# A feed-forward in written order: operands of a unit as one paced stream, weights that skip steps, low parts one step behind high parts

## The chip, the cores and the metric

The kernel runs on one core of one Trainium2 chip. The metric is the device time of one execution in microseconds. TensorE (PE) multiplies matrices; ScalarE (ACT), VectorE (DVE) and GpSimd (POOL) work on rows; SyncE (SP) issues the transfers (DMA). Each engine takes its instructions in the order in which they stand.

## What is computed

One layer of an encoder for 2048 prompt tokens and 32 sample tokens (2080 in all, 1024 channels): a mixing sub-layer (band attention beside gated linear attention), then a gated feed-forward with a causal convolution. All of the change lies in the feed-forward, which fills roughly the last 44% of the time:

```python
D_MODEL = 1024; D_FF = 2816; CONV_W = 3
...
def conv_ffn(h, conv_state, w_up, w_dw, b_dw, w_down):
    t = h.shape[1]
    u = h @ w_up                                       # (t, 2 * D_FF)
    uu = jnp.concatenate([conv_state.astype(u.dtype), u], axis=1)
    y = b_dw
    for j in range(CONV_W):
        y = y + w_dw[j] * uu[:, j:j + t]
    a, g = jnp.split(y, 2, axis=-1)
    out = (jax.nn.gelu(a, approximate=True) * g) @ w_down
    return out, uu[:, -(CONV_W - 1):]
```

All is float32.

## The kernel before

**Numbers in two parts.** A float32 operand is split into a high part (a copy rounded to a shorter format, made by ACT) and a low part (what is left, made by DVE as operand minus high part). A product is the sum of high·high, high·low and low·high on PE.

**Units and blocks.** The tokens are cut into three pairs of segments of about 348. The feed-forward has twelve *units*: u0, u1, u2 are the up-projection of one pair each, with 22 *blocks* of 128 channels; u3 to u11 are the down-projection, three groups for each pair, with 4 blocks each. A block is a 2×2 product done with seven multiplications (Strassen's scheme in Winograd's form). Its weights are named A11, S2, S1, S3, A12, S4, A22 and its operands (rows of tokens) B11, T2, T1, T3, B21, B22, T4; the S and T are sums of quarters. Each of the seven has four inner tiles of 128 (three in u5, u8 and u11) by three matmuls, so 12 (9) matmuls. The operands are the same for all blocks of a unit, the weights are new for each block.

**Steps.** After each multiplication `block` calls `side()`, a *step*. A step first runs what was put off until now (`run_due`), then makes one half of an operand of the next unit (`hstep`), then one of the coming weights (`next(wq)`), and a second if there is room in the ring of weights; last it drives the final part of an earlier pair (`pend`). The product A22·T4 of a block is written after A11·B11 of the next block.

**Order.** From the third block of u0 on, `in_order[0]` is true, and PE, ACT, DVE, POOL and SP take instructions in the order in which this Python code writes them. `put(n, f)` puts a piece of work off by n + 1 steps. So a high part is written in one step (L1464 for operands, L1540 for weights), and its low part (L1465, L1543) two steps later.

**Operands.** `load_ops` is a generator: it issues loads three halves ahead (L1323, L1440, L1444, L1447) into a few raw tiles `ht`, and each time that it is resumed it makes one high part and puts the low part off. The loads, from `h2T` and its sums `hT` (up) or from `actD` and its sums `aT` (down), wait on SP until a raw tile is free, which is once the low part was made from it. Operands of the next unit were asked for in three pieces:

```python
ahead_ = {14: [0], 17: [1], 21: range(2, 7)} if grp is None else {1: [0], 2: [1], 3: range(2, 7)}
if m in ahead_:
    hq.append(load_ops([(u + 1, OPS[i]) for i in ahead_[m]]))
```

that is B11 in block 14, T2 in block 17 and the other five in the last block (down-projection: blocks 1, 2 and 3).

**Weights.** `weights` loads quarters or stored sums (L1518) into ten raw slots, makes the high part, puts off the low part. In u0 and u3 to u5 the weights are *fresh*: the sums S are made on the chip, three on POOL (L1522) and S4 on DVE, and stored (L1546) for the later pairs.

**Rest.** L1597 is the matmul. L1705, L1713 and L1716 are ACT's copies of the results of A11·B11, S2·T2 (to U2) and S1·T1; L1719 and L1727 are DVE's additions after S3·T3 and S4·B22. L1612 and L1614 are the convolution. L1624 to L1627 (`act_sums`) make the T sums of the activations in every second block, L1647 multiplies by the gate, L1629 and L1648 store them. L1817 and L1821 are the last multiplication and addition of the output of an earlier pair, in u6 and u9.

Of the kernel before, what the change touches and what calls it, by code (L numbers as in the profile page):

```python
# [58 lines left out]
def encoder_step(ctx: ExitStack, tc: tile.TileContext, I, O):  # L59
# [1363 lines left out]
    def put(n, f):  # L1423

        later(n, f) if n and in_order[0] else f()

    def load_ops(todo):

        raws = {}

        def load(i):
            u, x, j, n = todo[i]
            p, g = UNITS[u]
            w = WIDTH[u]
            raws[i] = r = h_tile()
            if g is None and x in HB:
                k, s = HB[x]
                load_h(r, [(y, 4 * k + j + y, 2 * p + s) for y in range(2)], w)
            elif g is None:
                nc.sync.dma_start(r[:, :, :w], dap(hT, ((4 * p + HT[x]) * 512 + 128 * j) * W,  # L1440
                                                   [[W, 128], [128 * W, 2], [1, w]]))
            elif x in HB:
                k, s = HB[x]
                nc.sync.dma_start(r[:, :n, :w], dap(actD, ((p * MF + 8 * g + 2 * j + k) * 256 + s) * SEG,  # L1444
                                                    [[2 * SEG, 128], [512 * SEG, n], [1, w]]))
            else:
                nc.sync.dma_start(r[:, :n, :w], dap(aT, ((4 * p + HT[x]) * 11 + 4 * g + j) * 128 * SEG,  # L1447
                                                    [[SEG, 128], [128 * SEG, n], [1, w]]))

        todo = [(u, x, j, min(2, NK[u] - j)) for u, x in todo for j in (0, 2)]  # L1450
        for i in range(min(3, len(todo))):
            load(i)
        yield
        for i, (u, x, j, n) in enumerate(todo):
            if i + 3 < len(todo):
                load(i + 3)
            at = (7 * u + OPS.index(x)) % len(HP)
            assert HLIVE.setdefault(at, (u, x)) == (u, x)
            hi, lo = HP[at]
            if j:  # L1460
                put(1, lambda at=at, u=u, x=x: HO.update({(u, x): HP[at]}))
            w = WIDTH[u]
            hi, lo, r = hi[:, j:j + n, :w], lo[:, j:j + n, :w], raws.pop(i)[:, :n, :w]
            nc.scalar.activation(hi, r, AF.Copy)  # L1464
            put(1, lambda hi=hi, lo=lo, r=r: nc.vector.tensor_sub(lo, r, f32(hi)))  # L1465
            yield


# [2 lines left out]
    LIVE = {}  # L1471
# [33 lines left out]
    def weights():  # L1505
# [25 lines left out]
        def part(c, x, i):  # L1531
            u, m = cols[c]
            while True:
                place = ring((u, m, x))
                if place:
                    break
                yield
            n = NK[u]
            hi, lo = place
            nc.scalar.activation(hi[:, :n], raw(i, n), AF.Copy)  # L1540

            def low():
                nc.vector.tensor_sub(lo[:, :n], raw(i, n), f32(hi[:, :n]))  # L1543
                WO[u, m, x] = place
                if fresh[c] and x in SUM:
                    nc.sync.dma_start(w_rows(u, m, x), raw(i, n))  # L1546
                if fresh[c] and x == "A12":

                    def total4():
                        total(c, nc.vector, "tensor_sub", i, i, at[c, "S2"])  # L1550
                        at[c, "S4"] = i

                    put(1, total4)
                elif fresh[c] and x == "S2":
                    put(4, lambda: free.append(at.pop((c, "S2"))))
                else:
                    put(3 if fresh[c] and x in SUM else 1, lambda: free.append(i))

            put(1, low)

        fetch()
        for cur in range(len(cols)):
# [79 lines left out]
    def up_g(p, m, x, y, before):  # L1642

        o, c, d = WP[p] - 2, m + MF, int(p == 2)

        def act():
            nc.vector.tensor_mul(y[:, :, :o], y[:, :, :o], YG[:, :, :o])  # L1647
            put(2, lambda: nc.sync.dma_start(actD[p, m, :, :, :o], y[:, :, :o]))  # L1648
            if m % 2:
                made.append((p, m // 2, before, y))  # L1650

        if d:
            put(1, lambda: conv_outputs(x[:, 1], c))
        put(d + 1, lambda: tap(2, YG, x, c, o))
        put(d + 2, lambda: tap(1, YG, x, c, o))
        put(d + 3, lambda: tap(0, YG, x, c, o))
        put(d + 4, act)
# [171 lines left out]

            put(2, store)  # L1830

    pending = []

    def pend():
        while pending and next(pending[0], 1) == 1:
            pending.pop(0)
# [35 lines left out]
    YG = work[:, 8 * W:10 * W].rearrange("p (x w) -> p x w", w=W)  # L1872
    P5, U2 = work[:, 10 * W:11 * W], work[:, 11 * W:12 * W]

    def side():
        run_due()
        step()
        hstep()
        next(wq, None)
        if in_order[0] and len(LIVE) < len(RING) - 1:  # L1880

            next(wq, None)
        pend()
# [3 lines left out]
    for u, (p, grp) in enumerate(UNITS):  # L1887
        for m in range(NM[u]):
            if u == 0 and m >= 2 and ndone[0] == NBLK:
                ndone[0] += 1  # L1890
            if u + 1 < len(UNITS):

                ahead_ = {14: [0], 17: [1], 21: range(2, 7)} if grp is None else {1: [0], 2: [1], 3: range(2, 7)}
                if m in ahead_:
                    hq.append(load_ops([(u + 1, OPS[i]) for i in ahead_[m]]))
            if u == 3 and m == 1:
                nc.sync.dma_start(O["conv"], uc)
            if u == len(UNITS) - 1 and m == 2:
# [96 lines left out]
```

## Time and profile before

| | |
|---|---|
| median of 3 runs | 3315.63 us (3313.65 to 3321.91) |
| the profiled execution | 3320.35 us, its span 3318.4 us |
| PE busy | 3133.5 us, 94% of the span |
| DVE busy | 2269.8 us, 68% |
| ACT busy | 1650.5 us, 50% |
| POOL busy | 586.3 us, 18% |
| granted PE clock over the span | 0.979 |
| feed-forward | about 1850 to 3291 us of the span |

The shares are averages over the whole span; what an engine does in the feed-forward is read from its stretches. "Gap" below is time in which PE runs no matmul. An arrow in a row of waits means "waited for".

### The profile page before, as it was taken

How to read it: one execution, taken by the hardware profiler on the slowest of the kernel's cores; microseconds unless marked ns; L12 is line 12 of the kernel's file. 1: busy time of each engine (PE TensorE's matmuls, PEld its weight loads, DVE VectorE, ACT ScalarE, POOL GpSimd, SP SyncE). 2: the span in 40 equal slices, each digit the busy share in tenths (PEclk: the TensorE clock that was granted, in tenths of full speed). 3: DMA queues.
4: the chain of work that ended last, by engine and by line, in shares of the span. 5: the costliest groups of instructions: out<-in, count | busy, mean ns of one | idle time of the engine just before them, and what ended most of it. 6: DMA issues, size and time to landing. Idle time of an engine off the chain costs nothing. (4 is left out here: it accounts for less than half of the span.)

```text
span 3318.4 us, 57469 instructions
## 1 busy us (share of the span) xinstructions
PE 3133.5 (94%) x19928; PEld 2985.6 (90%) x19928; DVE 2269.8 (68%) x4858; ACT 1650.5 (50%) x3835; POOL 586.3 (18%) x687
## 2 busy tenths in 40 slices
PE   6999999999999999999999799999999999989996
PEld 4889998888999999889988789999999999989996
DVE  6725526674555555654776888987878788887876
ACT  4412224443544555543544645555555556575755
POOL 3102101111111111111444423300000001411011
PEclk9999999999999999999999899999999999999998
DMA  7344434445333333664575686676676666777774
GB/s 216 112 123 135 132 111 119 129 125 138 108 109 108 111 110 106 196 185 150 165 211 159 217 265 221 220 229 192 196 209 206 192 206 212 254 241 241 240 245 150
DMA packets 601365, 580.21 MB, mean 175 GB/s; under 512 B 55761, under 2 KB 529570, under 8 KB 601074
## 3 DMA queue, kind: packets, MB, share of 16 engines
q1 hardware_dynamic: 556386, 528.93, 53.2%
q10 hardware_dynamic: 44432, 47.34, 4.5%
q8 instruction: 157, 2.57, 0.3%
q14 instruction: 134, 1.10, 0.1%
q0 software_dynamic: 256, 0.26, 0.0%
HBM read 388.71 MB, written 187.65 MB: 174 GB/s over the span
## 5 line engine op out<-in xcount | busy, mean ns | idle before, releaser
L1597 PE MATMUL ad<-hA,hB 128*128 128x350 f32 (+2 forms) x1800 | 315.0, 325 | 9.3 <-DVE hB L1543 7.8
L1597 PEld LDWEIGHTS ad<-hA,hB 128*128 128x128 f32 x1800 | 294.6, 190 | 12.1 <-DVE hB L1543 9.2
L78 PE MATMUL pm<-hA,wh 128*128 128x416 f32 x768 | 288.8, 376 | 0.0
L1543 DVE TENSOR_TENSOR hA<-raws,hA 128x512 fp32r<-128x512 f32 (+1 forms) x360 | 270.1, 761 | 4.0 <-PE po L79 2.2
L79 PE MATMUL pm<-hA,wh 128*128 128x416 f32 x768 | 270.0, 352 | 0.0
L80 PE MATMUL pm<-hA,wl 128*128 128x416 f32 x768 | 269.8, 351 | 0.0
L1540 ACT ACTIVATE hA<-raws 128x512 fp32r<-128x512 f32 (+1 forms) x360 | 216.5, 615 | 54.7 <-PE ad L1597 13.8
L1597 PE MATMUL ad<-hA,hA 128*128 128x348 f32 (+2 forms) x1122 | 198.8, 328 | 9.7 <-DVE hA L1543 8.0
L938 POOL TENSOR_SCALAR P<-P,mx 128x640 f32<-128x640 f32 (+5 forms) x136 | 101.3, 745 | 546.5 <-DVE mx L937 260.9
L1597 PEld LDWEIGHTS ad<-hA,hA 128*128 128x128 f32 x1122 | 185.5, 192 | 11.8 <-DVE hA L1543 8.9
L1543 DVE TENSOR_TENSOR hB<-raws,hB 128x512 fp32r<-128x512 f32 (+1 forms) x269 | 196.1, 739 | 0.0
L1522 POOL TENSOR_TENSOR raws<-raws 128x512 f32<-128x512 f32 (+1 forms) x70 | 111.0, 1597 | 467.7 <-DVE hA L1543 347.7
L1597 PE MATMUL g<-hA,hB 128*128 128x348 f32 (+2 forms) x987 | 176.6, 329 | 18.1 <-ACT work L1713 11.0
L1597 PE MATMUL ad<-hA 128*128 128x350 f32 (+2 forms) x1101 | 191.1, 323 | 2.3 <-ACT work L1716 2.1
L1597 PEld LDWEIGHTS g<-hA,hB 128*128 128x128 f32 x987 | 163.5, 193 | 21.6 <-ACT work L1713 13.3
L1597 PEld LDWEIGHTS ad<-hA 128*128 128x128 f32 x1101 | 178.7, 189 | 3.9 <-ACT work L1716 3.6
L1705 ACT COPY g<-ad 128x348 f32<-128x348 f32 (+2 forms) x102 | 44.4, 435 | 276.9 <-PE ad L1597 230.2
L1540 ACT ACTIVATE hB<-raws 128x512 fp32r<-128x512 f32 (+1 forms) x269 | 163.3, 616 | 32.9 <-DVE raws L1522 14.2
L78 PE MATMUL pn<-wh,hA 128*128 128x256 f32 (+1 forms) x624 | 177.8, 285 | 0.0
L79 PE MATMUL pn<-wl,hA 128*128 128x256 f32 (+1 forms) x624 | 176.9, 283 | 0.0
L80 PE MATMUL pn<-wh,hA 128*128 128x256 f32 (+1 forms) x624 | 176.8, 283 | 0.0
L69 ACT ACTIVATE pth<-pp 128x256 fp32r<-128x256 f32 (+1 forms) x288 | 106.1, 373 | 127.0 <-PE pp L1005 115.8
(439 smaller groups left out, 9093.8 us busy)
## 6 DMA issues: line engine op xcount, KB each, us to landing
raws<-in_w_up_dram SPq DMA_DIRECT2D x220, 256.0 KB, 4.6
raws<-sW SPq DMA_DIRECT2D x176, 256.0 KB, 4.3
sW<-raws SPq DMA_DIRECT2D x88, 256.0 KB, 3.4
raws<-in_w_down_dram SPq DMA_DIRECT2D x80, 256.0 KB, 5.2
wr<-in_w_in_dram SPq DMA_DIRECT2D x76, 256.0 KB, 3.4
sgT<-tx ACTq DMA_DIRECT2D x80, 208.0 KB, 2.4
wa<-in_w_ada_dram SPq DMA_DIRECT2D x64, 256.0 KB, 3.0
keys<-ks SPq DMA_DIRECT2D x128, 128.0 KB, 2.9
```

The lines of the kernel that those rows point to most:

```text
L69: i = nc.scalar.activation(hi, src, AF.Copy)
L78: nc.tensor.matmul(out, ah, bh, start=first and i == 0, stop=False)
L79: nc.tensor.matmul(out, ah, bl, start=False, stop=False)
L80: nc.tensor.matmul(out, al, bh, start=False, stop=last and i == n - 1)
L938: nc.gpsimd.tensor_scalar(P[:m, :tot], P[:m, :tot], mx[:m, 6:7], 1.0, op0=OP.mult, op1=OP.mult)
L1522: getattr(eng, op)(raw(out, n), raw(a, n), raw(b, n))
L1540: nc.scalar.activation(hi[:, :n], raw(i, n), AF.Copy)
L1543: nc.vector.tensor_sub(lo[:, :n], raw(i, n), f32(hi[:, :n]))
L1597: nc.tensor.matmul(out[:, :w], l_[:, k], r_[:, k, :w], start=first and k == 0 and i == 0, stop=k == n - 1 and i == 2, skip_group_check=True)
L1705: nc.scalar.copy(g[:, 0, :w], ad[:, 0, :w])
```

## The change

Four things change, all in the order of instructions. `soon(n, f)` puts work off by one step less than `put(n, f)`, and the low parts of operands and weights, the sum S4, the freeing of raw slots and the store of activations now use it. `load_ops` is called once for each unit, for all seven operands, at block 18 of an up-projection and block 1 of a down-projection; it keeps two or three loads ahead, starts three steps after its first loads, makes two halves in three steps, and lets a step pass where the place of an operand is not yet free. `side()` makes no weight in every second step that made a half, if more than four weights are held, and no second weight in a step that made a half.

```diff
+    pending = []
+    made_half = [False]
+
+    def soon(n, f):
+
+        later(n - 1, f) if in_order[0] else f()
+
     def load_ops(todo):
...
         todo = [(u, x, j, min(2, NK[u] - j)) for u, x in todo for j in (0, 2)]
-        for i in range(min(3, len(todo))):
-            load(i)
-        yield
+        ahead = [0]
+
+        def more():
+
+            while ahead[0] < len(todo) and len(raws) < (2 if pending else 3):
+                load(ahead[0])
+                ahead[0] += 1
+
+        more()
+        for _ in range(3 if in_order[0] else 1):
+            yield
         for i, (u, x, j, n) in enumerate(todo):
-            if i + 3 < len(todo):
-                load(i + 3)
+            more()
+            if in_order[0] and i % 2 == 0:
+                yield
             at = (7 * u + OPS.index(x)) % len(HP)
-            assert HLIVE.setdefault(at, (u, x)) == (u, x)
+            while HLIVE.setdefault(at, (u, x)) != (u, x):
+
+                yield
+            made_half[0] = True
             hi, lo = HP[at]
             if j:
-                put(1, lambda at=at, u=u, x=x: HO.update({(u, x): HP[at]}))
+                soon(1, lambda at=at, u=u, x=x: HO.update({(u, x): HP[at]}))
             w = WIDTH[u]
             hi, lo, r = hi[:, j:j + n, :w], lo[:, j:j + n, :w], raws.pop(i)[:, :n, :w]
             nc.scalar.activation(hi, r, AF.Copy)
-            put(1, lambda hi=hi, lo=lo, r=r: nc.vector.tensor_sub(lo, r, f32(hi)))
+            soon(1, lambda hi=hi, lo=lo, r=r: nc.vector.tensor_sub(lo, r, f32(hi)))
             yield
...
-                    put(1, total4)
+                    soon(1, total4)
                 elif fresh[c] and x == "S2":
-                    put(4, lambda: free.append(at.pop((c, "S2"))))
+                    soon(4, lambda: free.append(at.pop((c, "S2"))))
                 else:
-                    put(3 if fresh[c] and x in SUM else 1, lambda: free.append(i))
-
-            put(1, low)
+                    soon(3 if fresh[c] and x in SUM else 1, lambda: free.append(i))
+
+            soon(1, low)
...
-            put(2, lambda: nc.sync.dma_start(actD[p, m, :, :, :o], y[:, :, :o]))
+            soon(2, lambda: nc.sync.dma_start(actD[p, m, :, :, :o], y[:, :, :o]))
...
+    turn = [False]
+
     def side():
         run_due()
         step()
+        made_half[0] = False
         hstep()
-        next(wq, None)
-        if in_order[0] and len(LIVE) < len(RING) - 1:
+        turn[0] ^= made_half[0]
+        if not (in_order[0] and made_half[0] and turn[0] and len(LIVE) > 4):
+            next(wq, None)
+        if in_order[0] and len(LIVE) < len(RING) - 1 and not made_half[0]:
 
             next(wq, None)
         pend()
...
-                ahead_ = {14: [0], 17: [1], 21: range(2, 7)} if grp is None else {1: [0], 2: [1], 3: range(2, 7)}
-                if m in ahead_:
-                    hq.append(load_ops([(u + 1, OPS[i]) for i in ahead_[m]]))
+                if m == (18 if grp is None else 1):
+                    hq.append(load_ops([(u + 1, x) for x in OPS]))
```

What this makes of the order is shown at three places. The lines of the changed kernel are 19 higher from `load_ops` on (the matmul L1597 is L1616, L1705 is L1724, L1465 is L1484, L1543 is L1562). `hA_104`, `hA_105`, `hB_677` and `ring` hold high and low parts, `raws` the raw weights, `ht` the raw operands, `work` the activations.

DVE in u0, the end of a block with the row sums L1624 to L1627; L1719 is the addition after S3·T3, L1727 the one after S4·B22. Before:

```order
L1719 TENSOR_TENSOR g<-g,work 128x350
L1614 SCALAR_TENSOR_TENSOR work<-g,cw,work 128x2x348
L1624 TENSOR_TENSOR work<-work 128x348
L1625 TENSOR_TENSOR work<-work 128x348
L1626 TENSOR_TENSOR work<-work 128x348
L1627 TENSOR_TENSOR work<-work 128x348
L1647 TENSOR_TENSOR work<-work 128x2x348
L1543 TENSOR_TENSOR hB_677<-raws,hB_677 128x512
L1543 TENSOR_TENSOR hA_105<-raws,hA_105 128x512
L1727 TENSOR_TENSOR ad<-ad,work 128x350
```

And now:

```order
L1738 TENSOR_TENSOR g<-g,work 128x350
L1633 SCALAR_TENSOR_TENSOR work<-g,cw,work 128x2x348
L1562 TENSOR_TENSOR hB_677<-raws,hB_677 128x512
L1643 TENSOR_TENSOR work<-work 128x348
L1644 TENSOR_TENSOR work<-work 128x348
L1645 TENSOR_TENSOR work<-work 128x348
L1646 TENSOR_TENSOR work<-work 128x348
L1666 TENSOR_TENSOR work<-work 128x2x348
L1562 TENSOR_TENSOR hB_677<-raws,hB_677 128x512
L1746 TENSOR_TENSOR ad<-ad,work 128x350
```

Before, no low part of a weight stands between the addition L1719 and the end of the sums, and two stand behind them, the second that of the next block's A11; now one stands ahead of the sums and one behind, and A11's was written six steps before its product instead of two.

ACT at the border of u0 and u1, in the first block of u1, from the copy of A11·B11 to the copy of S2·T2 (L1713). Before:

```order
L1705 COPY g<-ad 128x348
L1612 ACTIVATE work<-ad,cw 128x2x348
L1464 ACTIVATE hA_105<-ht 128x2x348
L1540 ACTIVATE hA_104<-raws 128x512
L1464 ACTIVATE hA_105<-ht 128x2x348
L1540 ACTIVATE hA_104<-raws 128x512
L1713 COPY work<-g 128x348
```

And now:

```order
L1724 COPY g<-ad 128x348
L1631 ACTIVATE work<-ad,cw 128x2x348
L1483 ACTIVATE hA_105<-ht 128x2x348
L1559 ACTIVATE ring<-raws 128x512
L1559 ACTIVATE hA_105<-raws 128x512
L1559 ACTIVATE hA_104<-raws 128x512
L1732 COPY work<-g 128x348
```

Two halves of operands and two weights stood between the two copies; now one half and three weights.

DVE at the same border, around the addition after S4·B22; the low parts into `hA_104` from `ht` are those of T4, the last operand. Before:

```order
L1614 SCALAR_TENSOR_TENSOR work<-g,cw,work 128x2x348
L1465 TENSOR_TENSOR hA_104<-ht,hA_104 128x2x348
L1543 TENSOR_TENSOR ring<-raws,ring 128x512
L1647 TENSOR_TENSOR work<-work 128x2x348
L1465 TENSOR_TENSOR hA_104<-ht,hA_104 128x2x348
L1543 TENSOR_TENSOR hB_677<-raws,hB_677 128x512
L1727 TENSOR_TENSOR ad<-ad,work 128x348
```

And now:

```order
L1666 TENSOR_TENSOR work<-work 128x2x348
L1562 TENSOR_TENSOR hA_104<-raws,hA_104 128x512
L1562 TENSOR_TENSOR hA_105<-raws_22894,hA_105 128x512
L1746 TENSOR_TENSOR ad<-ad,work 128x348
L1484 TENSOR_TENSOR hA_104<-ht,hA_104 128x2x348 x2
L1562 TENSOR_TENSOR hB_677<-raws,hB_677 128x512
```

Both low parts of T4 stood ahead of the addition that waits for S4·B22; now both stand behind it.

More of the change, by code (lines that the diff above doesn't have):

```diff
@@ L1830, in post @@
             put(2, store)
-    pending = []
     def pend():
```

## Prediction

> **What bounds the kernel now.** I read the windows of the feed-forward first, cut at the copy that follows each block's first product, so that a row is one unit (the first leaves out the blocks in which earlier work still ends). Then the waits of PE, then the timeline around the longest of them. Columns of the rows: stretch, its length, busy us with instruction counts for PE, PE's weight loads, DVE, ACT and POOL, granted PE clock, DMA share, GB/s.
>
> ```profile
> core 0: us, PE busy (x) PEld busy (x) DVE busy (x) ACT busy (x) POOL busy (x), PEclk, DMA share, GB/s
> 1927.30:2195.50 268.20, 251.29 (x1511) 248.34 (x1510) 246.16 (x338) 141.55 (x245) 78.50 (x58) 0.97 0.73 232
> 2195.50:2497.40 301.90, 297.50 (x1848) 296.63 (x1847) 243.44 (x367) 173.54 (x302) 0.00 (x0) 0.99 0.69 206
> 2497.40:2805.10 307.70, 300.09 (x1855) 299.22 (x1853) 251.57 (x412) 179.69 (x385) 6.27 (x8) 0.99 0.66 199
> 2805.10:2860.90 55.80, 54.38 (x326) 53.62 (x327) 49.84 (x66) 36.13 (x67) 21.88 (x11) 0.97 0.86 268
> 2860.90:2915.00 54.10, 53.76 (x335) 53.19 (x334) 44.23 (x61) 29.39 (x57) 19.15 (x12) 1.00 0.72 226
> 2915.00:2963.90 48.90, 44.74 (x267) 42.16 (x265) 46.35 (x69) 35.41 (x67) 11.40 (x9) 1.00 0.77 232
> 2963.90:3030.80 66.90, 56.04 (x340) 53.80 (x340) 54.91 (x69) 40.03 (x69) 15.24 (x8) 1.00 0.88 276
> 3030.80:3084.00 53.20, 52.71 (x323) 52.71 (x324) 33.51 (x55) 29.43 (x57) 0.00 (x0) 0.97 0.68 219
> 3084.00:3129.40 45.40, 43.69 (x267) 42.03 (x266) 38.91 (x64) 35.15 (x67) 0.00 (x0) 1.00 0.75 232
> 3129.40:3195.20 65.80, 57.23 (x340) 55.79 (x340) 55.23 (x69) 39.88 (x70) 14.51 (x8) 0.97 0.87 269
> 3195.20:3248.60 53.40, 52.92 (x322) 52.92 (x323) 33.58 (x55) 29.48 (x57) 0.00 (x0) 0.97 0.69 215
> 3248.60:3291.00 42.40, 41.20 (x256) 40.34 (x254) 31.05 (x54) 29.20 (x60) 0.70 (x14) 1.00 0.55 164
> 2300.00:2400.00 100.00, 99.84 (x624) 99.38 (x623) 79.76 (x122) 56.84 (x100) 0.00 (x0) 1.00 0.66 195
> ```
>
> The last row is steady work: 99.84/624 = 0.160 us a matmul, 13.44 us for a block of 84, 10.08 for one of 63. That is PE's floor, and the matmuls do not change. Length less floor, in order: u0 268.2 − 18 × 13.44 = 26.3; u1 301.9 − 295.7 = 6.2; u2 12.0; u3 2.0; u4 0.3; u5 48.9 − 40.3 = 8.6; u6 66.9 − 53.8 − 0.6 (four further matmuls) = 12.5; u7 none; u8 5.1; u9 11.4; u10 none; u11 2.1. Together 86 us is all that any reordering here can win.
>
> Who ends PE's waits (sum, times, longest):
>
> ```profile
> PE g L1597 <- ACT work L1713: 17.8, 12, 4.2
> PE g L1597 <- ACT g L1705: 15.1, 7, 4.8
> PE ad L1597 <- DVE hB L1543: 8.4, 6, 3.3
> PE ad L1597 <- DVE hA L1543: 8.0, 3, 5.5
> ```
>
> Low parts of weights (DVE) hold PE for 16.4 us; the 32.9 us behind ACT's copies are ACT being late, because it sat on something else.
>
> **The change part by part.** *Nothing is added to or taken from the arithmetic.* The same loads, high parts (ACT) and low parts (DVE) are issued in another order, so PE's and DMA's work is unchanged and only the excess can move.
>
> *Weights' low parts one step earlier.* In u0 every second block stalls at its first product:
>
> ```profile
> 2048.22 0.51 DVE L1624 TENSOR_TENSOR work<-work 128x348 f32<-128x348 f32 x1
> 2050.31 0.88 DVE L1647 TENSOR_TENSOR work<-work 128x696 f32<-128x696 f32 x1
> 2051.11 1.29 DVE L1543 TENSOR_TENSOR hA<-raws,hA 128x512 fp32r<-128x512 f32 x2
> 2051.85 1.88 PE L1597 MATMUL ad<-hA,hA 128*128 128x350 f32 x10 [0.86 <-DVE hA L1543]
> ```
>
> A11's low part stands behind four row sums and a product; they run from 2048.22 to 2051.2, longer than a product (12 × 0.16 = 1.93 us), and PE waits 0.86. With the order of the change the low part of A11 is issued 6 steps ahead of its product instead of 2, so three microseconds of sums no longer reach it. The bound is not u0's whole 26.3: DVE is busy 246.2 of 268.2, and no order makes it less, so 0 to 22.0. PE's two waits on low weights are 16.4 in all. I take 14: near the rows that name the wait, less two for a DVE that would then be busy 97%. The same shift elsewhere moves work between steps where DVE has slack (243.4 of 301.9): nothing, covered by that slack.
>
> *Operands in one stream, from block 18, two halves in three steps.* Before, the next unit's operands are made one half in each of the last and first steps:
>
> ```profile
> 2194.12 0.88 DVE L1465 TENSOR_TENSOR hA<-ht,hA 128x696 fp32r<-128x696 f32 x1
> 2195.51 0.52 DVE L1727 TENSOR_TENSOR ad<-ad,work 128x350 f32<-128x350 f32 x1
> 2197.52 0.85 SPq L1323 DMA_DIRECT2D ht<-h2T  x2
> 2202.61 0.79 ACT L1464 ACTIVATE hA<-ht 128x696 fp32r<-128x696 f32 x1 [1.83 <-DMA ht<-h2T]
> 2203.82 0.43 ACT L1713 COPY work<-g 128x348 f32<-128x348 f32 x1
> 2204.30 1.92 PE L1597 MATMUL g<-hA,hB 128*128 128x348 f32 x8 [4.25 <-ACT work L1713]
> ```
>
> The clock adds to such a gap:
>
> ```profile
> 2205.30:2208.70 3.40, 3.40 (x14) 3.40 (x13) 3.36 (x5) 1.31 (x3) 0.00 (x0) 0.50 1.10 302
> 2051.90:2055.30 3.40, 3.40 (x21) 3.40 (x22) 3.40 (x6) 1.29 (x2) 2.00 (x2) 1.00 0.62 227
> ```
>
> The first stretch follows the 4.25 us above, with 14 matmuls where 21 fit: 3.4 us at clock 0.50, so 1.7 us on top of the gap. The second follows the 0.86 us of u0 and costs nothing more. [...]
>
> ACT stands at the half of an operand until its load lands at 2202.6, about 4.3 us after SP issued it; the copy that PE needs is two instructions behind; PE waits 4.25 us. So the fault is the late issue, and that has a row too:
>
> ```profile
> SPq L1323 <- DVE hA L1465: 18.5, 5, 6.1
> ```
>
> SP holds such loads until a low part has freed a raw tile, up to 6.1 us. With low parts one step behind high parts the tile is free a step (1.93 us) sooner, more than the 1.83 us that ACT waited. Each of the three borders u0/u1, u1/u2, u2/u3 loses such a gap (longest rows 4.2 and 4.8) less its own step, with 1.7 us of clock: about 5.5 each, so at most 16.5.
>
> What this adds: the last operand T4 is now made late. Its two low parts stood ahead of the addition L1727, which waits for the S4 product; now they stand behind it. That product's end, + 0.52 + 0.88 + 0.88 = 2.3 us later the second half is there; it is needed one product and a half later (1.93 + 0.96 = 2.9). So it costs 0 while DVE is less than 0.6 us behind, and by the longest single foreign instruction ahead (0.88 above) or two, up to 1.5, otherwise. I take 1.5 at each border: 16.5 − 4.5 = 12, and 10 of it, since the loads still compete.
>
> *The same in the down-projection.* Blocks are few there and all seven operands are new every four blocks:
>
> ```profile
> ACT hA L1464 <- DMA ht<-actD: 27.7, 23, 2.5
> ACT hA L1464 <- DMA ht<-aT: 27.0, 18, 3.8
> SPq L1444 <- DVE hA L1465: 54.9, 24, 5.6
> ht<-aT SPq DMA_DIRECT2D x40, 348.0 KB, 5.2
> ```
>
> ACT waited 54.7 us for operand loads, which land 5.2 us after their issue; SP held them 54.9 us for free tiles. Excess sits at u5+u6 (115.8 us long) and u8+u9 (111.2). Taken as pairs, since the making of u6's operands falls into u5: DVE 46.35 + 54.91 = 101.3, PE's floor 94.7, DMA 0.77 × 48.9 + 0.88 × 66.9 = 96.5; so u5+u6 can win at most 14.5 (DVE). For u8+u9 the three are 94.1, 94.7 and 91.3, at most 16.5 (PE). Starting at block 1 and pacing over 21 steps spreads what was bunched, but in u5 and u8 a step is 9 × 0.16 = 1.44 us, three steps 4.3, and a load takes 5.2: some waiting of ACT stays. Between 0 and 31 I take half, 7 + 8 = 15.
>
> *POOL beside DVE.* In u6 and u9 the final additions of an earlier group run on POOL:
>
> ```profile
> 2998.57 0.68 DVE L1543 TENSOR_TENSOR hA<-raws,hA 128x512 fp32r<-128x512 f32 x1
> 2998.72 1.94 POOL L1821 TENSOR_TENSOR acc<-acc,ht 128x696 f32<-128x696 f32 x1 [2.02 <-DVE acc L1817]
> 2999.17 2.04 DVE L1543 TENSOR_TENSOR ring<-raws,ring 128x512 fp32r<-128x512 f32 x1
> ```
>
> A low part of 0.68 us takes 2.04 beside it. The change leaves these additions where they are, eight in each of the two units: that is the second reason for only half. [...]
>
> *Weights that give way.* Every second half-making step makes no weight if more than four are held, and none makes a second. Seven steps of 21 are skipped per border; PE consumes one a step, so the stock falls from about eight to four or five and refills afterwards. Four steps are 7.7 us: the stock hides the skipping. Fresh weights in u3 to u5 first need sums on DVE and POOL, which already hold ACT:
>
> ```profile
> ACT hB L1540 <- DVE raws L1522: 13.2, 7, 4.0
> ```
>
> Cost 0 to two such waits (2 × (4.0 + 1.7) = 11.4). I take 2: the mean wait is 13.2/7 = 1.9 us, one step, and four steps are in stock. Raw weights freed earlier let SP's loads start earlier; in u7, u10, u11 that is +1. The blocks before 1927, where the order was not yet fixed by hand, have the same instructions: nothing, and 3 us either way in the range.
>
> **Sum.** 14 + 10 + 15 + 1 − 2 = 38 us. The profiled execution took 3320.35 (span 3318.4 and 2 around it), so 3282; the median of the runs, 3315.63, lies 4.7 below it, so 3278. A difference below 0.3%, 10 us, cannot be told from none.
>
> **Rivals.**
> *DVE, POOL and DMA stay the bound.* u0 then wins half (7), u5 to u9 only 4 (POOL's eight additions still stretch DVE, DMA's share is 0.88 there), borders 7: 18 in all, 3298. For it: DVE at 92% in u0, waits of ACT on loads that three short steps don't cover. Against it: in u8 DVE is busy only 38.9 of 45.4, and POOL not at all, and 5.1 us are lost.
> *All of the bounded losses go.* 22 in u0, 14 at the borders, 24 in u5 to u9: 60, 3256. Against it: two engines would be at 97% and more.
> *Weights starve at u3 to u5.* 11.4 us where I took 2: 3287. For it: seven waits of ACT on POOL's and DVE's sums exist already.
> *Slower: the last operands come late at each border.* Only two loads run ahead of the half being made instead of three. If T4's load, at the end of the stream, lands a step late, ACT stands with the copies of the next product behind it, and PE waits as at 2204.30. At 3.5 us and 1.7 of clock for each of the eleven borders it costs 57 against 40 gained: +17, 3333. It decides from 40/11 = 3.6 us a border, clock included. Against it: T4 has 2.9 us of slack after S4, and its load is issued at least three steps ahead (5.8, in short steps 4.3, against 5.2).
> *Nothing moves*, since ACT's waits are on DMA that is as late as before: u0's gain is then eaten by T4's, within 10 us of 3316.
>
> **Chances.** The forecast 0.50 (3268 to 3290 on its own), DVE and POOL 0.20, starving 0.10, all gone 0.10, nothing 0.06, slower 0.04. The first four are faster by over 0.3%: 0.90; same 0.06; slower 0.04. The range reaches from 3256 (all gone) to 3302 (4 us past the DVE rival) and leaves out the last two cases and a tail below.
>
> **What would show it.** In u0 the 0.86 us gaps before every second block's A11 gone, PE's waits on L1562 (the old L1543) below 5 us and DVE above 95%; u0's 18 blocks in about 254 us. At the three borders no PE gap over 3 us and no stretch at clock 0.50; SP's waits for operand tiles at less than half of 54.9. u5+u6 near 109, u8+u9 near 103; ACT's waits for actD and aT near 30. Wrong it would be if PE's waits move to the low part of T4 or B22 (L1484), if the first blocks of u4 to u11 each show a gap of over 2 us, or if DVE in u0 does not rise: then the order wasn't the cause of the lost time there.

## The result and the profile after

The changed kernel takes 3288.9 us (median of 4 runs, 3285.18 to 3291.58) against 3317.09 for the kernel before (4 runs, 3313.65 to 3321.91: the three of the table above and one more): a ratio of 0.9913, 95% interval 0.9896 to 0.9931. It is faster by 28 us; 38 were forecast (3278, range 3256 to 3302).

The windows of the changed kernel, cut at the same copies (now L1724), u0 without its first four blocks, then u1, u2, u3, u5, u6, u8, u9; columns as before:

```profile
1926.33:2188.45 262.12, 248.26 (x1511) 246.52 (x1510) 252.78 (x341) 141.43 (x241) 72.59 (x56) 0.98 0.81 249
2188.45:2485.79 297.34, 296.13 (x1850) 295.55 (x1849) 242.23 (x367) 173.23 (x300) 0.14 (x2) 1.00 0.75 206
2485.79:2785.92 300.13, 298.96 (x1858) 298.40 (x1857) 247.82 (x409) 180.10 (x385) 6.60 (x6) 1.00 0.72 202
2785.92:2847.84 61.92, 55.72 (x330) 53.82 (x329) 54.22 (x70) 36.16 (x68) 20.15 (x13) 0.97 0.80 248
...
2902.16:2946.15 43.99, 42.60 (x260) 41.03 (x259) 42.62 (x67) 34.81 (x66) 7.76 (x6) 1.00 0.85 264
2946.15:3010.41 64.26, 57.33 (x349) 56.48 (x347) 51.12 (x68) 40.20 (x68) 13.30 (x8) 0.97 0.84 271
...
3063.99:3105.45 41.46, 41.46 (x260) 40.97 (x259) 37.35 (x63) 34.41 (x66) 0.00 (x0) 1.00 0.83 252
3105.45:3166.98 61.53, 56.55 (x349) 55.39 (x347) 52.30 (x68) 40.22 (x68) 14.24 (x8) 1.00 0.90 274
```

Against the rows of before: u0 −6.1, u1 −4.6, u2 −7.6, u3 **+6.1**, u5 −4.9, u6 −2.6, u8 −3.9, u9 −4.3. The four units not shown change by less than 1.5 each (u11 taken to PE's last matmul, as in the table below). Two things stand out. In u0 DVE is busier than before (252.8 against 246.2), with three more instructions. And u3 got longer.

What PE waits for in the changed kernel (sum, times, longest):

```profile
PE g L1616 <- ACT work L1732: 18.9, 7, 5.7
PE g L1616 <- DVE hA L1484: 5.9, 6, 2.6
PE g L1616 <- ACT g L1724: 4.1, 2, 2.1
```

The 16.4 us for low parts of weights are gone (L1562 appears only with 1.6 and less). ACT's copy of S2·T2 (L1732) still ends 18.9 us of waiting, in 7 cases. Some lines of the timeline of u0 around the longest:

```profile
1955.43 0.52 DVE L1349 TENSOR_TENSOR ht<-ht 128x348 f32<-128x348 f32 x1
1956.00 3.05 POOL L1541 TENSOR_TENSOR raws<-raws 128x512 f32<-128x512 f32 x2 [0.99 <-DVE ht L1349]
1956.42 1.49 DVE L1644 TENSOR_TENSOR work<-work 128x348 f32<-128x348 f32 x1
1957.94 1.48 DVE L1645 TENSOR_TENSOR work<-work 128x348 f32<-128x348 f32 x1
1961.29 0.52 DVE L1746 TENSOR_TENSOR ad<-ad,work 128x350 f32<-128x350 f32 x1
1961.85 0.93 ACT L1631 ACTIVATE work<-ad,cw 128x696 f32<-128x696 f32 x1 [8.60 <-DVE ad L1746]
1963.72 0.44 ACT L1732 COPY work<-g 128x350 f32<-128x350 f32 x1
1964.21 2.12 PE L1616 MATMUL g<-hA,hB 128*128 128x350 f32 x6 [5.67 <-ACT work L1732]
```

Two of the four sums of activations (L1643 to L1646) take 1.49 instead of 0.52 while two sums of POOL (L1541) run beside them, and the sums of operands of the next pair (to L1349) stand just ahead. So DVE reaches the addition L1746 late, ACT's convolution (L1631) waits 8.60 us for it, the copy that PE needs stands behind that, and PE waits 5.67 us; over the next 3.4 us the granted clock is 0.58. A second stall of 5.53 us follows two blocks later, with 3.4 us at 0.50 behind it. After that most blocks of u0 take 13.51, where every second one took 14.65.

The kernel before has stalls at the same place, under another name. There the same eight sums stand ahead of the low part of the next A11, and it is this low part that ends PE's wait:

```profile
1951.04 0.52 DVE L1346 TENSOR_TENSOR ht<-ht 128x348 f32<-128x348 f32 x1 [0.75 <-DMA ht<-h2T]
1953.11 0.52 DVE L1349 TENSOR_TENSOR ht<-ht 128x348 f32<-128x348 f32 x1
1955.64 0.88 DVE L1647 TENSOR_TENSOR work<-work 128x696 f32<-128x696 f32 x1
1956.43 1.29 DVE L1543 TENSOR_TENSOR hA<-raws,hA 128x512 fp32r<-128x512 f32 x2
1957.17 2.12 PE L1597 MATMUL ad<-hA,hA 128*128 128x350 f32 x6 [5.51 <-DVE hA L1543]
```

Here POOL is idle beside the sums, and DVE waits for two loads instead. The two blocks that hold such stalls took 19.61 and 19.65 us before; the two of the changed kernel take 20.71 and 22.03.

In u3 the same pair of engines meets at T4, whose two low parts now stand behind the addition:

```profile
2802.23 0.52 DVE L1746 TENSOR_TENSOR ad<-ad,work 128x348 f32<-128x348 f32 x1
2804.05 2.76 DVE L1484 TENSOR_TENSOR hA<-ht,hA 128x696 fp32r<-128x696 f32 x2
2804.35 3.59 POOL L1541 TENSOR_TENSOR raws<-raws 128x512 f32<-128x512 f32 x2 [3.19 <-DVE raws L1541]
2804.98 1.22 PE L1616 MATMUL g<-hA 128*128 128x348 f32 x6 [2.64 <-DVE hA L1484]
```

Two low parts that need 0.87 each take 2.76 beside POOL; PE waits 2.64, and a further 0.67 for the second half, and from 2806.8 on its clock is 0.50 for 3.4 us.

### The profile page after: what moved, and what is told of

The parts are those of the page before. It is cut to its first block, busy times and chain, and to the rows that moved or that the text cites. A ratio compares the mean times of both kernels' runs of the same rounds, so it can differ in the third digit from the quotient of the medians.

```text
span 3289.9 us, 57758 instructions
## 1 busy us (share of the span) xinstructions
PE 3122.5 (95%) x19928; PEld 2977.8 (91%) x19928; DVE 2267.6 (69%) x4858; ACT 1650.9 (50%) x3835; POOL 579.6 (18%) x687
## 5 line engine op out<-in xcount | busy, mean ns | idle before, releaser
L1616 PE MATMUL ad<-hA,hB 128*128 128x348 f32 (+2 forms) x1791 | 311.3, 324 | 1.2 <-ACT work L1735 0.7
L1616 PEld LDWEIGHTS ad<-hA,hB 128*128 128x128 f32 x1791 | 292.7, 190 | 1.8 <-ACT work L1735 1.0
L1562 DVE TENSOR_TENSOR hA<-raws,hA 128x512 fp32r<-128x512 f32 (+1 forms) x355 | 256.2, 731 | 10.8 <-ACT hA L1559 10.3
L1616 PE MATMUL g<-hA,hB 128*128 128x350 f32 (+2 forms) x1044 | 187.1, 329 | 19.4 <-ACT work L1732 17.0
L1562 DVE TENSOR_TENSOR hB<-raws,hB 128x512 fp32r<-128x512 f32 (+1 forms) x271 | 198.5, 736 | 5.5 <-ACT hB L1559 5.4
L938 POOL TENSOR_SCALAR P<-P,mx 128x640 f32<-128x640 f32 (+5 forms) x136 | 101.3, 745 | 548.0 <-DVE mx L937 269.6
L1616 PE MATMUL ad<-hA 128*128 128x350 f32 (+2 forms) x1119 | 195.3, 324 | 1.9 <-DVE hA L1562 1.6
L1616 PEld LDWEIGHTS g<-hA,hB 128*128 128x128 f32 x1044 | 173.2, 193 | 22.6 <-ACT work L1732 19.4
L1616 PEld LDWEIGHTS ad<-hA 128*128 128x128 f32 x1119 | 182.8, 190 | 2.6 <-DVE hA L1562 1.9
L1616 PE MATMUL g<-hA 128*128 128x350 f32 (+2 forms) x975 | 172.9, 327 | 11.4 <-ACT work L1732 6.8
L1541 POOL TENSOR_TENSOR raws<-raws 128x512 f32<-128x512 f32 (+1 forms) x69 | 101.0, 1472 | 459.4 <-DMA raws<-in_w_down_dram 307.3
L1616 PE MATMUL ad<-hA,hA 128*128 128x350 f32 (+2 forms) x1020 | 178.5, 324 | 1.0 <-DVE hA L1484 0.5
L1616 PEld LDWEIGHTS g<-hA 128*128 128x128 f32 x975 | 160.1, 191 | 14.4 <-ACT work L1732 7.6
```

The costliest lines, as they stand in the source:

```text
L938: nc.gpsimd.tensor_scalar(P[:m, :tot], P[:m, :tot], mx[:m, 6:7], 1.0, op0=OP.mult, op1=OP.mult)
L1541: getattr(eng, op)(raw(out, n), raw(a, n), raw(b, n))
L1616: nc.tensor.matmul(out[:, :w], l_[:, k], r_[:, k, :w], start=first and k == 0 and i == 0, stop=k == n - 1 and i == 2, skip_group_check=True)
```

## The experiments

Theory at the start: three parts of the change each win in their own place. The shorter delay of low parts wins u0, the stream wins the borders and u5 to u9, skipping weights costs u3, and POOL beside DVE holds the rest. The table has the length of each stretch (us, cut at the copy of A11·B11, u0 without four blocks, u11 to PE's last matmul), from the one profiled execution of each kernel, and the ratio to the kernel before from the timed runs.

| kernel | ratio (95%) | u0 | u1+u2 | u3+u4 | u5+u6 | u8+u9 | u7+u10+u11 |
|---|---|---|---|---|---|---|---|
| before | 1 | 268.2 | 609.7 | 109.9 | 115.8 | 111.2 | 155.3 |
| changed | 0.9913 (0.9896–0.9931) | 262.1 | 597.5 | 116.2 | 108.3 | 103.0 | 154.9 |
| low parts only | 0.9936 (0.9919–0.9953) | 263.9 | 603.3 | 111.4 | 109.2 | 108.4 | 153.1 |
| operands' low parts only | 0.9947 (0.9932–0.9961) | 266.0 | 602.7 | 108.6 | 113.0 | 106.9 | 154.7 |
| the same, loads two ahead | 0.9973 (0.9962–0.9984) | 263.9 | 611.6 | 108.7 | 112.3 | 106.2 | 154.3 |
| stream and skipping, old delays | 1.0062 (1.0045–1.0080) | 273.5 | 607.9 | 127.4 | 118.3 | 107.0 | 158.8 |
| stream alone, old delays | 1.0087 (1.0069–1.0105) | 268.6 | 611.3 | 122.7 | 123.5 | 111.8 | 161.6 |
| changed, no skipping | 0.9947 (0.9930–0.9964) | 263.7 | 600.2 | 114.4 | 112.3 | 107.5 | 156.9 |
| changed, small POOL work | 0.9852 (0.9814–0.9890) | 252.2 | 596.5 | 111.3 | 103.0 | 101.3 | 155.0 |
| changed, POOL's work on DVE | 0.9872 (0.9854–0.9891) | 254.6 | 596.9 | 112.9 | 107.5 | 102.8 | 154.9 |

**The shorter delays alone.** The kernel before, with `soon` in the seven places of the diff and nothing else.

> The kernel before, with only the shorter delays (low parts, S4, freed raw slots and the store of activations one step earlier); operands are still asked for in three pieces and weights never skip. Theory: the shorter delay alone wins what the change won in u0 (from 268.2 to about 262) and little elsewhere; the long gaps at the borders stay (first block of u1 18, of u2 19, last of u2 18 us), u5+u6 stays above 112: about 8 us faster, ratio 0.9975. Rival: the raw operand tiles that come free a step earlier already remove the borders' gaps, and the stream adds nothing: about 20 us faster, ratio 0.994.

Measured: 0.9936. The rival's figure, and the larger part of the whole gain: not only u0 (263.9, as the theory had it) but the borders and u5 to u9 get shorter, without any stream.

**The stream and the skipping, with the old delays.**

```diff
     def soon(n, f):
 
-        later(n - 1, f) if in_order[0] else f()
+        later(n, f) if in_order[0] else f()
```

> The changed kernel with the old delays (low parts two steps behind high parts); the stream of operands and the skipping of weights stay. Theory: the borders' gaps and u5 to u9 win as in the changed kernel (u1+u2 about 598, u5+u6 109), u0 goes back to 268 with a stall of 0.86 in every second block: about 20 us faster than before, ratio 0.994. Rival: with low parts a step later, T4 and B22 come too late at each of the eleven borders (1 to 3 us each, some with a stretch at half clock): no more than 5 us faster, ratio 0.9985 or above.

Measured: 1.0062, slower than before; the theory fell and even the rival was too kind. From the end of u3 to the start of u6 PE waits for weights:

```profile
PE ad L1616 <- DVE hA L1562: 5.7, 4, 2.1
PE ad L1616 <- DVE hB L1562: 4.8, 3, 2.3
```

**The stream alone, with the old delays.** The last kernel, and besides:

```diff
-        if not (in_order[0] and made_half[0] and turn[0] and len(LIVE) > 4):
-            next(wq, None)
-        if in_order[0] and len(LIVE) < len(RING) - 1 and not made_half[0]:
+        next(wq, None)
+        if in_order[0] and len(LIVE) < len(RING) - 1:
```

> The changed kernel with the old delays and without skipping of weights: the stream of operands alone. The stream with skipping and old delays was 0.6% slower than before, with PE waiting 1.7 us for a weight's low part in nearly every block of u3 to u5. Theory: the skipping takes the stock of weights down, and with low parts two steps behind it doesn't hold; without skipping u3+u4+u5 fall from 179 to about 160, and the stream alone is about 5 us faster than before: ratio 0.9985. Rival: the late T4 and B22 make the stream itself slow; u3+u4+u5 stay above 172 and the ratio above 1.003.

Measured: 1.0087; u3 to u5 together 174.9. The waits for weights are gone from the same stretch, as the theory said; but T4's low part has taken their place:

```profile
PE g L1616 <- DVE hA L1484: 7.0, 3, 3.7
PE ad L1616 <- DVE hA L1562: 0.4, 1, 0.4
```

The second blocks of u3, u4 and u5 take 22.4, 19.9 and 18.1 us: the rival, in both its figures. So the slower rival of the prediction, last operands late at each border, is a real cost of the stream, and one step of delay decides whether it bites. Its mechanism is another than the prediction gave: there ACT stood at T4's load, while here, from the end of u3 to the start of u6, ACT waits only 2.4 us for operand loads, and what comes late is the low part on DVE.

**Operands' low parts one step earlier, alone.** The kernel before, with `soon` only in the two places of `load_ops`.

> The kernel before, with only the low parts of operands one step earlier; weights and the rest keep the old delays. Theory: what the shorter delays won outside u0 (12 us of 20) comes from raw operand tiles that are free a step earlier, so that SP issues the next loads earlier: u1+u2 from 610 to 604, u5+u6 from 116 to 110, u0 stays at 268: 11 us faster, ratio 0.9965. Rival: it comes from weights that are made and stocked earlier: under 4 us faster, ratio above 0.9985.

Measured: 0.9947, most of the gain of all shorter delays, with u0 unchanged in kind (every second block 14.65) and u1+u2 7 us shorter, as the theory had it. u5+u6 won 2.8, half of what it said, and u8+u9 4.3. ScalarE's waits for operand loads, all its rows together, fall from 80 to 50 us.

**The same, with loads two halves ahead.**

```diff
-        for i in range(min(3, len(todo))):
+        for i in range(min(2, len(todo))):
             load(i)
...
-            if i + 3 < len(todo):
-                load(i + 3)
+            if i + 2 < len(todo):
+                load(i + 2)
```

> The kernel before, with the low parts of operands one step earlier (which alone gave 0.9947), and loads two halves ahead instead of three. A raw tile's load is then written where its tile is long free, but is issued a step later against the half that needs it, as it was in fact before, when SP held it until the low part had freed the tile; the low parts stay early. Theory: the early low parts won because loads start earlier; with two ahead the gain goes: ratio 0.9985 or above, ScalarE's waits for operand loads back from 50 to about 80 us. Rival: they won because the low parts are in time for their products, whatever the loads do: ratio 0.996 or below.

Measured: 0.9973, between the two, and the stretches say why. Windows of u1 and u2, first with loads three ahead, then two:

```profile
2189.82:2487.79 297.97, 296.78 (x1850) 295.50 (x1849) 243.87 (x367) 173.11 (x300) 0.13 (x2) 1.00 0.70 208
2487.79:2792.49 304.70, 299.57 (x1860) 298.70 (x1858) 252.18 (x414) 179.47 (x385) 6.60 (x7) 1.00 0.67 202
```

```profile
2178.44:2480.51 302.07, 297.94 (x1850) 297.08 (x1849) 244.26 (x367) 173.45 (x301) 0.14 (x2) 0.99 0.69 204
2480.51:2790.07 309.56, 301.04 (x1860) 300.17 (x1858) 251.89 (x414) 179.47 (x385) 6.36 (x7) 0.99 0.66 199
```

At the borders of the up-projection the gain is gone (611.6 against 602.7; before, 609.7), and ACT's rows at the border of u0 and u1 show a late load there, first with three ahead, then with two:

```profile
2197.04 0.79 ACT L1468 ACTIVATE hA<-ht 128x696 fp32r<-128x696 f32 x1 [0.58 <-DMA ht<-hT]
```

```profile
2188.78 0.78 ACT L1468 ACTIVATE hA<-ht 128x696 fp32r<-128x696 f32 x1 [3.66 <-DMA ht<-hT]
```

This load was issued 4.25 us after the unit's first copy, against 3.16, and landed 6.1 us after its issue, against 4.1; PE's copy stands behind it, and PE waits 3.95 us instead of 0.85. So in the up-projection the early low part won because the load started earlier.

In the down-projection all of the gain stays (u3 to u11 481.5 against 483.3; before, 492.1), and ACT's waits for loads, over all units, stay at 52 us instead of going back to 80. But this doesn't show that an earlier load is not the reason there. The loads of the down-projection are issued as early with two ahead as with three: for u5 the first four of actD go out 7.2, 6.8, 3.8 and 2.4 us ahead of the unit's first copy, with three ahead 7.2, 6.7, 3.8 and 1.8, and in the kernel before 7.2, 4.2, 3.4 and 0.5. The edit didn't delay them, since SP still holds them until a low part has freed a tile (35.3 us in 22 cases). Whether the earlier loads or the low parts' own time win in the down-projection was not told apart. (The profiled execution was the shortest of this kernel's, for the part ahead of the feed-forward ran 9 us ahead; the stretches leave that part out.)

**No skipping of weights.** The changed kernel with `side()` as it was.

> The changed kernel in which weights never skip a step and a second weight is made as before. Theory: u3, which the change made 6 us longer (61.9), was starved of weights by the skipping and falls to about 56; the rest is as in the changed kernel: 3283, 0.2% faster than it. Rival: u3's loss comes from VectorE stretched by GpSimd, and from T4's low parts behind the S4 addition; u3 stays at 60 or more, and the borders get longer since ACT makes more in the same steps: 3289 to 3295.

Measured: 0.9947 against 0.9913 for the changed kernel. u3 falls by 2.2, not 6, and u6 and u9 rise by 4 each:

```profile
2945.42:3013.96 68.54, 58.38 (x347) 57.25 (x346) 50.15 (x69) 40.79 (x69) 13.31 (x8) 0.95 0.78 258
3110.05:3175.34 65.29, 56.36 (x348) 55.15 (x346) 52.89 (x68) 40.60 (x69) 13.75 (x8) 0.99 0.89 268
```

Skipping is no cost, and without it the stream adds nothing to the short delays alone (0.9936). The intervals with and without it only just touch. That it wins by taking weights off ScalarE and SP in the steps in which operands are made is the likely reason, but no run shows it.

**Less work on POOL.** The changed kernel with POOL's sums on one inner tile and its last additions on 64 columns (inside the ordered part). The rest of this work is left out, so it prices POOL's share and is no kernel to use.

```diff
-            n = NK[cols[c][0]]
+            n = NK[cols[c][0]] if eng is nc.vector or not in_order[0] else 1
...
-            add.tensor_add(a, a, xs.pop(m)[:, :, :o])
+            e = o if final else 64
+            add.tensor_add(a[:, :, :e], a[:, :, :e], xs.pop(m)[:, :, :e])
```

> The changed kernel in which GpSimd does a part of its work in the ordered feed-forward: the three sums of fresh weights on one of four (three) inner tiles, the last additions of the output of the first two pairs on 64 of 348 columns; what it leaves out is missing from the output. Theory: what still holds u0, u3, u6 and u9 is VectorE stretched by GpSimd (50 us of VectorE time in u0): u0 from 262 to about 248, u3 to 57, u6 to 58, u9 to 57: about 25 us faster than the changed kernel, 3264. Rival: GpSimd only runs beside, the waits are of order and transfers: less than 6 us faster.

Measured: 0.9852, 20 us faster than the changed kernel. u0 in the window:

```profile
1926.56:2178.75 252.19, 246.85 (x1514) 245.97 (x1513) 222.35 (x340) 142.43 (x241) 30.25 (x56) 0.99 0.85 257
```

DVE does nearly the same instructions (340, in the changed kernel 341) in 222 us instead of 253. The 50 us of stretched DVE time that the expectation names is too much: measured against the shortest of each shape, the DVE instructions of u0 take some 38 us too long in the changed kernel and 7 in this one. The theory holds in u0 (−10), u3 (−4.6), u6 (−3.6) and u9 (−1.8).

**POOL's work on DVE.** Nothing left out:

```diff
+        def T3_():
+            return nc.vector if in_order[0] else nc.gpsimd
...
-            total(c, nc.gpsimd, "tensor_add", s1, a21, at[c, "A22"])
-            total(c, nc.gpsimd, "tensor_sub", s2, s1, at[c, "A11"])
-            total(c, nc.gpsimd, "tensor_sub", a21, at[c, "A11"], a21)
+            total(c, T3_(), "tensor_add", s1, a21, at[c, "A22"])
+            total(c, T3_(), "tensor_sub", s2, s1, at[c, "A11"])
+            total(c, T3_(), "tensor_sub", a21, at[c, "A11"], a21)
...
-            add = nc.vector if final and i % 2 else nc.gpsimd
+            add = nc.gpsimd if final and i % 2 == 0 else nc.vector
```

> The changed kernel in which VectorE does what GpSimd did in the ordered feed-forward: the three sums of fresh weights and the last additions of the first two pairs. Theory: a sum of 1.5 us on GpSimd stretches VectorE beside it by about as much as VectorE needs to do it (0.68), so nothing is lost: u0 within 8 us of 262, u6 and u9 3 us shorter, ratio to before 0.991 +- 0.003. Rival: on VectorE the sums also wait for their weights' transfers, with low parts queued behind: u0 over 275, slower than the changed kernel by 15 us or more.

Measured: 0.9872, better than the theory dared; its interval does not overlap that of the changed kernel, and it beats both kernels. The gain is in u0 (−7.5) and u3 (−3.0); u6 and u9, which the theory had 3 us shorter, stay. u0 in the window:

```profile
1921.29:2175.94 254.65, 247.12 (x1514) 246.24 (x1513) 247.23 (x391) 142.43 (x241) 0.79 (x8) 0.99 0.83 254
```

DVE does 50 instructions *more* than in the changed kernel (391 against 341) and is busy 5.6 us *less*.

**Four variants around it.** First, the operand sums moved away from the activation sums, and a faster stream (`i % 4` for `i % 2`), on the changed kernel:

> The changed kernel with two edits that act in different stretches. (1) The sums of operands of the next pair (four operations of VectorE) wait a step where the sums of activations (four more) were just written. Theory: the two blocks of 20.7 and 22.0 us in u0 come from these eight operations ahead of the S4 addition, which ScalarE's queue waits for: u0 from 262 to about 252. Rival: GpSimd beside VectorE alone makes them: over 259. (2) The stream makes four halves in five steps instead of two in three. Theory: T4's wait of 0.6 to 2.6 us in the second block of u1 to u5 goes, 5 us in all over u1 to u11; rival: the loads are no longer ahead, ACT waits for them, and the first blocks of u6 and u9 get longer: up to 10 us lost there.

Measured: 0.9925, no gain. u0 258.3 (a stall in block 7 remains, 22.6), nearer to the rival than to the theory; u1+u2 595.4 with T4's waits mostly gone, but u6 70.9 and u9 68.1: both the theory on T4 and the rival on loads came true, and the second is larger. Of the two paces, two halves in three steps is the better one in u6 and u9.

The move of the operand sums alone, with POOL's work on DVE:

> The changed kernel with GpSimd's sums and additions on VectorE (the version that was 0.4% faster than the changed kernel), and the operand sums of the next pair a step later where activation sums were just written. Theory: u0's three remaining stalls (blocks of 18.0, 15.6 and 18.3) are these operations ahead of the S4 addition: u0 from 254.6 to about 247, ratio to before 0.985. Rival: the stall only moves to the next step, as it did with GpSimd at work: within 3 us of 3272, ratio 0.987.

Measured: 0.9871 (0.9851 to 0.9891), u0 254.5: the rival. The stall moves a block on.

The shorter delays and POOL's work on DVE, without stream and skipping:

> The kernel before with all shorter delays (0.9936), and with GpSimd's sums and additions on VectorE, so without the stream and without skipping. Theory: moving GpSimd's work is worth the same 14 us there (u0, u3, u6, u9), and the stream with skipping a further 7: 3284 or ratio 0.990, 0.3% behind the version with the stream. Rival: with VectorE no longer stretched the stream brings nothing: ratio 0.987 as with it.

Measured: 0.9918 (0.9903 to 0.9933); u0 257.0, u8+u9 110.0. The stream with skipping is worth 0.5% here: the theory, and more of it than was expected. The other half of the theory missed: against the short delays alone (0.9936) moving POOL's work wins 6 us and not 14, and the intervals overlap.

And a delay of none for the operands' low parts, with POOL's work on DVE:

> The changed kernel with GpSimd's work on VectorE, and the low part of an operand written in the same step as its high part (delay 0; it was 2 before, 1 in the change; weights keep 1). Theory: what the delay does is free raw tiles and bring T4 in time; T4's waits of 0.3 to 0.8 us in the second blocks of u1 to u5 go, and u6 and u9 get their loads earlier: 5 us faster than 3272, ratio 0.9855. Rival: VectorE now waits for each high part (0.8 us and what ScalarE is behind) with everything after it: borders get longer, over 3280, ratio 0.9895 or above.

Measured: 0.9861 (0.9839 to 0.9883), within the uncertainty of 0.9872 with a delay of one. The theory came in part at most: PE's waits for T4's low part in the second blocks go in u4 and u5, but grow from 0.7 to 1.5 and 1.3 in u1 and u2 and from 0.6 to 2.2 in u3, and the first blocks of u6 and u9 grow from 13.3 to 14.5. From two steps to one wins 0.5%; from one to none wins nothing that can be told.

## Why the prediction was right, and where not

The sign was right and the total within the range: 28 of 38 us. By the stretches the 28 are 6.1 in u0, 12.2 in u1 and u2, −6.3 in u3 and u4, 7.5 in u5 and u6, 8.1 in u8 and u9 and 0.4 in the rest. Step by step:

- **Low parts of weights in u0: 14 forecast, 6 measured.** This is the term that failed, by its size. It was taken near the 16.4 us of the two rows, but the waits for low parts of weights in u0 (16.7 us, with those into `ring`) are of two kinds. Six short ones (0.86 five times, 1.65 once: 6.0 us) are of the kind whose timeline the prediction showed; they went, all but one of 0.58, and that is about what u0 won. Three long ones (5.51, 1.91 and 3.29: 10.7 us) stand where sums of operands or of activations pile up on DVE, some of them waiting for loads. Writing A11's low part earlier doesn't shorten these sums: PE now waits there for the next thing behind them, the addition L1746 and ACT's copy, 5.67 and 5.53 us. DVE did rise to 96%, but in part by stretching: the prediction took DVE's 246.2 us for a fixed amount of work, but the new order raised them by 6.6, and with little POOL work nearly the same instructions took 222.
- **The borders: 10 forecast; u1+u2 gave 12.2, u3 took 6.1 back.** The last operands cost 0.5 and 0.7 us at u1 and at u2, below the 1.5 charged, and 2.6 + 0.7 at u3, with POOL beside it, and then 3.4 us at half clock, which the prediction's signs had ruled out at the borders. The stretching was in the text for u6 and u9, but not carried over to u3, where POOL's fresh sums also run. (Of the two longest rows that the text took for borders, the one of 4.8 us stands between u6 and u7; the three borders lost 4.25, 3.81 + 0.87 and 3.46.) The cause given for the gain, raw tiles that come free a step sooner, is what the run with loads two ahead shows for the up-projection; the credit to the stream was wrong: with the old delays it wins next to nothing there.
- **u5 to u9: 15 forecast (7 and 8), 7.5 and 8.1 measured.** Right in size, and the reason for taking half (loads against three short steps, POOL) is seen: ACT still waits 17.0 us for aT. But it takes all three parts together: the operands' low parts alone give 7, all short delays 9, the stream without skipping 7.
- **Skipping weights: forecast to cost 2; it wins 0.3%.** Priced only as a loss of stock; what it may free on ACT and SP was left out.
- **"SP's waits for operand tiles at less than half"** was a wrong sign to look for:

```profile
SPq L1454 <- DVE hA L1484: 71.0, 36, 8.3
SPq L1451 <- DVE hA L1484: 38.3, 18, 5.0
ACT hA L1483 <- DMA ht<-aT: 17.0, 6, 5.5
ACT hA L1483 <- DMA ht<-actD: 4.3, 4, 2.2
```

L1451 and L1454 are the old L1444 and L1447. SP waits longer, which fits loads that are written earlier, against tiles still in use; what matters fell: ACT's waits for actD and aT, from 54.7 to 21.3.
- **Rivals.** 28 lies halfway between the forecast (38) and the rival with DVE and POOL as the bound (18), and the parts divide: u0 (6.1) and the borders (6.1 net) came out as the rival had them (7 and 7), u5 to u9 (15.6) as the forecast had it (15, rival 4). That the total is inside the range is in part luck. The slower rival is what the stream does with the old delays. Starving at u3 is 2.2 of the 6.1.

## What to carry to other kernels

A low part, or any step whose end frees a buffer that a load waits for, is priced also by the load that it lets start, and not only by its own time: one step earlier for the operands alone was worth 0.5% here, and the elaborate stream around it was a loss without it. The parts of such a change are not additive; run each alone before crediting it. A row that sums waits can hold several kinds of wait: look at each long one before taking the row as what an edit can win, for a wait that is removed at one instruction can come back at the next one behind the same work. And before an engine's busy time is used as a floor, check whether its instructions are stretched by a neighbour: work off-loaded to POOL was not free, and taking it back was worth another 0.4% in the changed kernel (0.2%, within the uncertainty, without the stream).

## What the hardware showed

A sum of 128x512 took a median of 1.36 us on POOL and 0.68 on DVE; the row of each kind, first the changed kernel, then the one with POOL's work on DVE:

```profile
L1541 POOL TENSOR_TENSOR raws<-raws x69: 1008/1356/2383, 1822.0 to 2926.0; 128x512 f32<-128x512 f32 x61, 128x384 f32<-128x384 f32 x8
```

```profile
L1541 DVE TENSOR_TENSOR raws<-raws x78: 547/684/695, 1825.1 to 2911.2; 128x512 f32<-128x512 f32 x68, 128x384 f32<-128x384 f32 x10
```

By these medians a sum took 1.98 times as long on POOL as on DVE.

One of the sums of activations on DVE, in both kernels (L1643 in the first is L1646 in the second), shows what POOL's sums add: its longest is three times its shortest in the first, and none is stretched in the second (shortest/median/longest in ns):

```profile
L1643 DVE TENSOR_TENSOR work<-work x33: 503/514/1612, 1893.5 to 2817.0; 128x348 f32<-128x348 f32 x22, 128x346 f32<-128x346 f32 x11
```

```profile
L1646 DVE TENSOR_TENSOR work<-work x33: 508/514/518, 1890.2 to 2800.8; 128x348 f32<-128x348 f32 x22, 128x346 f32<-128x346 f32 x11
```

Beside POOL's sums in u0, DVE's additions L1644 and L1645 took 1.49 and 1.48 instead of 0.52 us, so a sum on POOL could cost DVE about 1.0 us (an estimate from these times), more than the 0.68 of doing it: with 50 more operations on DVE in u0, DVE's busy time there was 5.6 us lower. Not expected was that the stretching makes the off-loading a net loss: with POOL's work on DVE the ratio was 0.9872 against 0.9913.

PE's clock fell after shorter waits than the 4.25 us of the prediction. In u0 of the kernel before, PE waited 1.91 us (at 1988.97); the stretch of 3.4 us around that wait, and the one after it:

```profile
1986.90:1990.28 3.38, 1.47 (x10) 1.31 (x9) 3.25 (x7) 0.00 (x0) 0.45 (x1) 1.00 0.88 272
1990.28:1993.68 3.40, 3.40 (x14) 3.40 (x13) 3.33 (x6) 1.04 (x2) 0.82 (x1) 0.50 0.50 183
```

PE was busy 1.47 of 3.38 us, and the next 3.4 us ran at half clock, with 14 matmuls. At the 0.160 us of steady work these take 2.24, so the half clock cost about 1.2 us beside the wait of 1.91: an estimate from these counts. The prediction's 1.7 is half of its 3.4 us; its stretch also holds 14 matmuls, so by the same count it is 1.2.
